# Seven-product matrix multiplication in another order: low halves last, one more chunk by seven products, and more low parts fetched by DMA

## The chip, the core and the metric

The kernel runs on one core of a Trainium2 chip. The core has five engines, each with an in-order stream of instructions of its own: TensorE (matrix products; in the profile PE, its weight loads PEld), VectorE (DVE), ScalarE (ACT), GpSimd (POOL) and SyncE (SP, which here only issues DMAs). They work side by side and wait for each other by semaphores. The metric is the device time of one execution in microseconds; lower is better.

## The reference

A trunk of two layers over 512 tokens of width 1024: layer 0 mixes tokens by gated linear attention, layer 1 by softmax attention. After each comes the part that the change is about:

```python
def conv_ffn(h, w_up, w_conv, b_conv, w_down):      # h 512 x 1024, w_up 1024 x 5632, w_down 2816 x 1024
    u = h @ w_up
    u = lax.conv_general_dilated(
        u, w_conv[:, None, :], window_strides=(1,), padding=[(1, 1)],
        dimension_numbers=('NWC', 'WIO', 'NWC'), feature_group_count=u.shape[-1]) + b_conv
    val, gate = jnp.split(u, 2, axis=-1)
    return (jax.nn.silu(gate) * val) @ w_down

...
        x = x + conv_ffn(rmsnorm(x, norm_ffn[i]), ffn_w_up[i], ffn_w_conv[i],
                         ffn_b_conv[i], ffn_w_down[i])
```

## The kernel before

**Numbers in two halves.** TensorE multiplies a reduced-precision type (fp32r). So every float32 operand is split into a high part, the value rounded to fp32r, and a low part, what is left. A product takes three matmuls: high weight by high input, high weight by low input, low weight by high input. `split` (L311 on) makes the high part on ScalarE (L319) and the low part on VectorE (L320). `low_dma` (L270 on) does it otherwise: ScalarE writes the high part (L271) and the negated value into the low tile (L272), and a DMA from GpSimd's queue adds the original values to it. The DMAs wait in `self.pending` until `flush` (L304 on) issues them (L308). Their source is the tile in the core's own memory or, where `home` is given, the same values in HBM.

**Pieces of weights.** The weights of a feed-forward layer are read in pieces of 128 x 1024 (512 KB) by SyncE. `W.todo` lists them in order; `made` holds those already split. `piece` flushes, makes what it was asked for if that has not been done, then makes up to `ahead` pieces in advance (`PA` = 4, or `PAW` = 6 from chunk 1 to chunk 19, when the tiles of x lend their space) and returns the one asked for. The program only states dependences and an order of writing; the order in which each engine gets its instructions is settled by a scheduler when the kernel is built.

**Chunks.** The 22 chunks of the up projection have 128 values and 128 gates each: two tiles of 128 x 512 results. In a plain chunk (`plain_up`, L1041) each tile is 8 x 3 matmuls of 512 columns. In the chunks of `SEVEN` the two tiles together are computed by Winograd's form of Strassen's scheme: seven products in place of eight, on blocks of half the size. `product` (L1065) is one of the seven: four block pairs, three matmuls of 256 columns each (L1074). Products 1 to 7 use sums of weight blocks, which `summed` (L275 on) makes: the first piece of a strip (half 0) is the stored one and serves products 1 and 4, the second (half 1: L293, L294) serves 6 and 2, the third 7 and 5, and the fourth, of half the size (L283 to L286), serves 3. `LOW_0` lists the chunks whose first piece gets its low part by `low_dma` out of HBM; elsewhere `split` makes it.

**Order of a chunk by seven products** (`seven_up`, L1083). Product 1 goes to a bank of its own (r1 in `pt`) and ScalarE doubles it (`twice`, L1129) into the bank `both`; the chunk pauses there until its predecessor has come far enough. Then: product 6 on top in r2; a copy of r2 to the first half of r3 (L1095, or L1204 in the down projection); product 7 to r4, doubled to `d`; product 4 on top of r3's first half; product 5 on top of r2; a copy of r2 to r3's second half (L1102, L1211); the sum of `d` and r3 on VectorE (L1132), which is the gate tile. Then product 1 of the next chunk, products 2 and 3, and the value tile is `both` itself. `act_up` (L1110) takes each tile through the convolution (L1117 to L1119), SiLU (L1121) and their product (L1122).

**The down projection** works in two parts of four strips (`down_part`, L1182) after chunks 9 and 17 (`DOWN_AFTER`), with the same products in the same order; its results are added to x in HBM by GpSimd's DMAs (`xd`). The rest of it (chunks 16 to 21, `PLAIN`) runs as plain products at the end. `prepare` (L1141 to L1157) builds the sums of the activations for it, for each pair of chunks up to 15.

**At the head of each feed-forward layer** the first three chunks use inputs not yet divided by the norm; `rescale` (L1029) prepares the others: xr (L1035), its high part nh, its low part nl by `low_dma` with xr as source.

Of the kernel before, what the change touches and what calls it, by code (L numbers as in the profile page):

```python
# [14 lines left out]
P = 128  # L15
# [54 lines left out]
SEVEN = (6, 7, 8, 10, 11, 12, 13, 15, 16, 18, 19, 20, 21)  # L70
UPA = 3
PA = 4
# [5 lines left out]
LOW_0 = (7, 8)  # L78
# [22 lines left out]
def hybrid_encoder_kernel(  # L101
# [74 lines left out]
    class Weights:  # L176
# [127 lines left out]
        def flush(self):  # L304

            for lo, r in self.pending:
                same = lo.dtype == F32R and r.dtype != F32R
                pool.dma_start(lo.bitcast(F32) if same else lo, r, accum_op=ALU.add)  # L308
            self.pending = []
# [40 lines left out]
    def add_ffn(layer):  # L350
        first = 0
        for m, part in DOWN_AFTER.items():
# [3 lines left out]
            W.todo[at : at + 2] = W.todo[at + 1], W.todo[at]  # L356
# [660 lines left out]
    def ffn(layer, norm, cw, nxt):  # L1017
# [11 lines left out]
        def rescale():  # L1029

            for p in range(KC // 2):
# [5 lines left out]
                W.low_dma(hi, lo, xr)  # L1037
                scaled.append(xr)
                fresh.extend((hi[:, i * S : (i + 1) * S], lo[:, i * S : (i + 1) * S]) for i in range(2))

        def plain_up(m):  # L1041

            pss = []
            for t in range(2):
# [3 lines left out]
                if t == 0 and m not in DOWN_AFTER:  # L1048
                    begin_up(m + 1)
                if t == 0 and m in DOWN_AFTER:  # L1050
                    down.append(down_part(DOWN_AFTER[m], m))
                    next(down[-1])
# [12 lines left out]
        def product(pieces, src, strip, pairs, i, dst, start):  # L1065
            h, o = PLACE[i]
            if h not in pieces:
                pieces[h] = W.piece(src, strip, h, PAW if W.wide else PA)
            wh, wl = pieces[h]
            for j, p in enumerate(pairs):  # L1070
                sl = slice(o + j * P, o + (j + 1) * P)
                mh, ml = p[i]
                for a, (w, m) in enumerate(((wh, mh), (wh, ml), (wl, mh))):
                    mm(dst, w[:, sl], m, start=start and j == 0 and a == 0, stop=j == len(pairs) - 1 and a == 2,  # L1074
                       skip_group_check=True)
# [6 lines left out]

        def seven_up(m):  # L1083
# [3 lines left out]
            r = bank("pt", "r1")[:, :H]  # L1087
            go(1, r, True)
            both = bank("acc", "r")
            r1, r2 = both[:, :H], both[:, H:]  # L1090
            twice(both, r)
            yield
            go(6, r2, False)
            r3 = bank("s", "r3")
            act.activation(r3[:, :H], r2, AF.Copy)  # L1095
# [6 lines left out]
            act.activation(r3[:, H:], r2, AF.Copy)  # L1102
            add_seven(d, r3, r4)
            yield 1, d
            begin_up(m + 1)
            go(2, r1, False)
# [75 lines left out]
        def down_part(part, m):  # L1182
# [6 lines left out]
            go = lambda n, *a: product(pieces[n], w_dn, part * NQ + n, pairs, *a)  # L1189

            def begin(n):
# [407 lines left out]
```

## Time and profile before

| | us |
|---|---|
| median of 3 runs | 1087.01 |
| lowest and highest | 1086.85, 1087.84 |
| span of the profiled execution, first to last instruction | 1085.5 |
| TensorE busy | 1077.5 |
| VectorE busy | 888.5 |
| ScalarE busy | 721.1 |
| GpSimd busy | 136.7 |

The profile is one execution recorded by the hardware. A group's row gives line, engine, operation, output and inputs by the program's names, shapes and count, then after a bar the busy time in us and the mean in ns of one, and after a second bar the idle time of the engine before them and what ended it. A row of waits says which engine waited at which line for which other, the total in us, the number of times and the longest. A row of a timeline has the start and the length in us, and in brackets the engine's idle time before it. Matmuls run into each other: the recorded length of one is more than the step to the next. Feed-forward layer 0 runs from 217.9 to about 562 us of the span, layer 1 from 735.7 us to the end. TensorE's granted clock is full (1.00) but for the last stretch.

### The profile page before, as it was taken

Reading aid. Unit: us, or ns where it says so; the run is one execution under the profiler, and the core shown is the slowest. Engines: PE = TensorE matmul, PEld = TensorE weight load, DVE = VectorE, ACT = ScalarE, POOL = GpSimd, SP = SyncE. Lnnn points to the kernel's source line nnn. Section 1 sums busy time; section 2 is a strip of 40 time slices with the busy share of each in tenths; the row PEclk is TensorE's granted clock in tenths of the full one; section 3 lists DMA queues with packets and bytes.
Section 4 is the critical chain, followed back from the end, with each engine's and each line's share of the span. In section 5 each row is a group of like instructions: output and inputs, shape, how many; then the busy total and the mean of one; then the engine's idle time right before and its main releaser. Section 6 shows DMA issues by size and latency. Waiting matters only on the chain.

```text
span 1085.5 us, 17391 instructions
## 1 busy us (share of the span) xinstructions
PE 1077.5 (99%) x6672; PEld 966.4 (89%) x6672; DVE 888.5 (82%) x1327; ACT 721.1 (66%) x1134; POOL 136.7 (13%) x153
## 2 busy tenths in 40 slices
PE   9999999999999999999999999999999999999998
PEld 8888988888999999999988888888889999999997
DVE  7998967569898899988755588666989889998882
ACT  8679575478775676666574677656877567666660
POOL 0212112021001100010015333002110010001000
PEclk9999999999999999999999999999999999999999
DMA  8744446499545633274767475549863473227542
GB/s 301 187 126 106 122 141 215 154 207 204 127 125 127 145 120 111 77 177 121 252 149 162 127 204 164 164 158 202 206 148 124 105 166 116 100 80 157 136 175 78
DMA packets 55763, 164.52 MB, mean 152 GB/s; under 512 B 6528, under 2 KB 7040, under 8 KB 55680
## 3 DMA queue, kind: packets, MB, share of 16 engines
q1 hardware_dynamic: 36192, 112.66, 32.2%
q0 software_dynamic: 14592, 42.21, 21.7%
q10 hardware_dynamic: 4896, 8.55, 2.1%
q8 instruction: 52, 0.85, 0.3%
q14 instruction: 31, 0.25, 0.1%
HBM read 114.89 MB, written 14.68 MB: 119 GB/s over the span
## 4 chain that ended last, share of the span: by engine, by line
PE 87%; DVE 6%; ACT 3%; DMA 2%; issue 2%; POOL 0%; SPq 0%; DVEq 0%; ACTq 0%; POOLq 0%
PE r L1074 37%; PE op L535 8%; PE vg L652 7%; PE up L482 4%; PE up L483 4%; PE up L484 4%; PE dn L483 2%; PE dn L484 2%; PE dn L482 2%; PE av L509 1%; PE A L482 1%; DVE wl L320 1%; PE A L484 1%; DMA nl<-xr 1%; PE B L484 1%
## 5 line engine op out<-in xcount | busy, mean ns | idle before, releaser
L320 DVE TENSOR_TENSOR wl<-raw,wh 128x1024 fp32r<-128x1024 f32 x156 | 189.8, 1220 | 31.3 <-ACT wh L319 31.1
L319 ACT ACTIVATE wh<-raw 128x1024 fp32r<-128x1024 f32 x156 | 162.6, 1053 | 73.4 <-PE op L535 20.7
L1074 PE MATMUL r<-gu,wh 128*128 128x256 f32 x896 | 161.2, 282 | 0.0
L1074 PE MATMUL r<-xt,wh 128*128 128x256 f32 x832 | 151.1, 283 | 0.4 <-ACT r L1095 0.3
L1074 PEld LDWEIGHTS r<-gu,wh 128*128 128x128 f32 x896 | 139.3, 190 | 1.0 <-ACT r L1211 0.2
L1074 PEld LDWEIGHTS r<-xt,wh 128*128 128x128 f32 x832 | 129.2, 190 | 1.6 <-ACT r L1095 1.1
L1074 PE MATMUL r<-gu,wl 128*128 128x256 f32 x448 | 126.3, 283 | 0.0
L1074 PE MATMUL r<-xt,wl 128*128 128x256 f32 x416 | 117.2, 283 | 0.0
L1074 PE MATMUL r<-nh,wh 128*128 128x256 f32 x312 | 88.8, 285 | 0.3 <-ACT r L1102 0.3
L1074 PE MATMUL r<-nh,wl 128*128 128x256 f32 x312 | 88.2, 283 | 0.0
L1074 PE MATMUL r<-nl,wh 128*128 128x256 f32 x312 | 87.9, 282 | 0.0
L1074 PEld LDWEIGHTS r<-gu,wl 128*128 128x128 f32 x448 | 85.1, 190 | 0.0
L1074 PEld LDWEIGHTS r<-xt,wl 128*128 128x128 f32 x416 | 79.1, 190 | 0.0
L482 PE MATMUL up<-nh,wh 128*128 128x512 f32 x192 | 75.3, 392 | 0.0
L483 PE MATMUL up<-nl,wh 128*128 128x512 f32 x192 | 75.2, 392 | 0.0
L484 PE MATMUL up<-nh,wl 128*128 128x512 f32 x192 | 75.2, 392 | 0.0
L535 PE MATMUL op<-oT,wh 128*128 128x512 f32 x256 | 72.4, 393 | 0.0
L271 ACT ACTIVATE wh<-raw 128x1024 fp32r<-128x1024 f32 x36 | 38.0, 1056 | 38.2 <-PE up L483 11.5
L1074 PEld LDWEIGHTS r<-nh,wh 128*128 128x128 f32 x312 | 59.3, 190 | 2.9 <-ACT r L1102 2.6
L1074 PEld LDWEIGHTS r<-nl,wh 128*128 128x128 f32 x312 | 59.4, 190 | 0.2
L1074 PEld LDWEIGHTS r<-nh,wl 128*128 128x128 f32 x312 | 59.4, 190 | 0.0
L535 PEld LDWEIGHTS op<-oT,wh 128*128 128x128 f32 x256 | 47.4, 188 | 9.7 <-ACT oT L937 0.3
(299 smaller groups left out, 2761.6 us busy)
## 6 DMA issues: line engine op xcount, KB each, us to landing
raw<-in_w_up_dram SPq DMA_DIRECT2D x84, 512.0 KB, 4.6
raw<-in_w_down_dram SPq DMA_DIRECT2D x44, 512.0 KB, 3.7
wl<-raw POOLq DMA_DIRECT2D x20, 512.0 KB, 5.3
wl<-in_w_up_dram POOLq DMA_DIRECT2D x16, 512.0 KB, 7.8
ring<-p ACTq DMA_DIRECT2D x32, 256.0 KB, 2.6
xw<-in_xw_dram SPq DMA_DIRECT2D x8, 512.0 KB, 6.6
raw<-in_w_v_dram SPq DMA_DIRECT2D x8, 512.0 KB, 5.9
raw<-in_w_g_dram SPq DMA_DIRECT2D x8, 512.0 KB, 4.0
```

Of the source, the lines that this page charges most:

```text
L271: act.activation(hi, r, AF.Copy)
L319: act.activation(hi[:, sl], a, AF.Copy)
L320: dve.tensor_tensor(lo[:, sl], a, hi[:, sl].bitcast(F32), ALU.subtract)
L482: mm(ps, wh, mh, start=start, stop=False)
L483: mm(ps, wh, ml, start=False, stop=False)
L484: return mm(ps, wl, mh, start=False, stop=stop)
L509: mm(ps[j][:, :width], hl[k][i == 2][:, j * P : (j + 1) * P], (wl if i == 1 else wh)[:, sl], start=k == 0 and i == 0, stop=k == KC - 1 and ...
L535: mm(pss[ng][n], wt[:, sl], mv, start=k == late[0][0] and i == 0, stop=k == late[-1][-1] and i == 2)
L652: last = mm(ps[j], m[:, js], w[:, sl], start=i in (1, 7, 2) and p == 0 and a == 0, stop=i in (4, 2, 3) and p == 3 and a == 2, skip_group_c ...
L1074: mm(dst, w[:, sl], m, start=start and j == 0 and a == 0, stop=j == len(pairs) - 1 and a == 2, skip_group_check=True)
```

## The change

Four things are changed, all in the feed-forward layers.

1. `product` runs its matmuls in another order: first both matmuls with the high weight for all four block pairs, then the four with the low weight. A copy out of the product's bank (`then`) is written straight after the matmuls, and only after it the making of further pieces, which had stood before them.
2. The seven products run in the order 1, 6, 7, 2, 5, (product 1 of the next chunk or strip), 4, 3 in place of 1, 6, 7, 4, 5, (next 1), 2, 3.
3. Chunk 14 joins `SEVEN` (its weights are laid out for it in HBM as those of the others), and chunks 11 to 16 join `LOW_0`.
4. `rescale` issues the DMAs of the low parts one by one, each behind the last DMA that had been sent before.

```diff
-SEVEN = (6, 7, 8, 10, 11, 12, 13, 15, 16, 18, 19, 20, 21)
+SEVEN = (6, 7, 8, 10, 11, 12, 13, 14, 15, 16, 18, 19, 20, 21)
...
-LOW_0 = (7, 8)
+LOW_0 = (7, 8, 11, 12, 13, 14, 15, 16)
...
-                pool.dma_start(lo.bitcast(F32) if same else lo, r, accum_op=ALU.add)
+                self.sent = pool.dma_start(lo.bitcast(F32) if same else lo, r, accum_op=ALU.add)
...
         def rescale():
 
+            W.flush()
+            sent = W.sent
             for p in range(KC // 2):
...
                 W.low_dma(hi, lo, xr)
+                with tc.issue_after(sent.ins):
+                    W.flush()
...
-        def product(pieces, src, strip, pairs, i, dst, start):
+        def product(pieces, src, strip, pairs, i, dst, start, then=None):
             h, o = PLACE[i]
             if h not in pieces:
-                pieces[h] = W.piece(src, strip, h, PAW if W.wide else PA)
+                pieces[h] = W.piece(src, strip, h, 0)
             wh, wl = pieces[h]
-            for j, p in enumerate(pairs):
-                sl = slice(o + j * P, o + (j + 1) * P)
-                mh, ml = p[i]
-                for a, (w, m) in enumerate(((wh, mh), (wh, ml), (wl, mh))):
-                    mm(dst, w[:, sl], m, start=start and j == 0 and a == 0, stop=j == len(pairs) - 1 and a == 2,
-                       skip_group_check=True)
+            steps = [(j, wh, a) for j in range(len(pairs)) for a in range(2)]
+            steps += [(j, wl, 0) for j in range(len(pairs))]
+            for n, (j, w, a) in enumerate(steps):
+                mm(dst, w[:, o + j * P : o + (j + 1) * P], pairs[j][i][a], start=start and n == 0,
+                   stop=n == len(steps) - 1, skip_group_check=True)
+            if then is not None:
+                then()
+            W.ahead((PAW if W.wide else PA) - len(W.made))
             W.flush()
...
+        def begin(m):
+            if m in DOWN_AFTER:
+                down.append(down_part(DOWN_AFTER[m], m))
+                next(down[-1])
+            else:
+                begin_up(m + 1)
+
         def seven_up(m):
...
-            go(6, r2, False)
             r3 = bank("s", "r3")
-            act.activation(r3[:, :H], r2, AF.Copy)
+            go(6, r2, False, copy(r3[:, :H], r2))
             r4 = bank("pt", "r4")[:, :H]
-            go(7, r4, True)
             d = tmp("u", "u")
-            twice(d, r4)
+            go(7, r4, True, lambda: twice(d, r4))
+            go(2, r1, False)
+            go(5, r2, False, copy(r3[:, H:], r2))
+            begin(m)
             go(4, r3[:, :H], False)
-            go(5, r2, False)
-            act.activation(r3[:, H:], r2, AF.Copy)
             add_seven(d, r3, r4)
             yield 1, d
-            begin_up(m + 1)
-            go(2, r1, False)
             go(3, r2, False)
             yield 0, both
```

`down_part` is changed in the same way; there the sum `f` of a strip is appended to `W.pending` after product 4 of that strip. `copy(o, i)` is ScalarE's copy of i to o.

More of the change, by code (lines that the diff above doesn't have):

```diff
@@ L1047, in plain_up @@
                 pss.append(ps)
[L1048 to L1052 removed]
+                if t == 0:
+                    begin(m)
                 if m == 0 and t == 0:
```

42 lines of the change are left out of this document (19 added, 23 removed).

## The prediction

> **What bounds the kernel now.** I read the page first: span, busy line, chain.
>
> ```profile
> span 1085.5 us, 17391 instructions
> ...
> PE 1077.5 (99%) x6672; PEld 966.4 (89%) x6672; DVE 888.5 (82%) x1327; ACT 721.1 (66%) x1134; POOL 136.7 (13%) x153
> ...
> PE 87%; DVE 6%; ACT 3%; DMA 2%; issue 2%; POOL 0%; SPq 0%; DVEq 0%; ACTq 0%; POOLq 0%
> ```
>
> TensorE has work for 99% of the span and carries 87% of the chain that ended last. Matmuls overlap, so busy time does not say how dense they are. The chain in order of time does: a piece's length by its count is the step from one matmul to the next.
>
> ```profile
> 187.83 30.26 PE op L535 x133
> ...
> 328.18 75.90 PE r L1074 x636
> ...
> 847.23 76.13 PE r L1074 x636
> ```
>
> L1074 is the matmul of the products, 256 columns: 75.90/636 = 119.3 ns, in layer 1 119.7 ns. A plain projection moves 512 columns; chunk 14's own matmuls, from the TensorE timeline (first and last of 13 in a row):
>
> ```profile
> 409.42 0.39 PE L484 MATMUL up<-nh,wl 128*128 128x512 f32 x1
> ...
> 412.14 0.39 PE L484 MATMUL up<-nh,wl 128*128 128x512 f32 x1
> ```
>
> 2.72 us over 12 steps: 226.7 ns. Neither step can be shortened by the other engines; all that can go is matmuls and the pauses between them. The waits of the weight loads list the pauses in the products:
>
> ```profile
> PEld r L1074 <- ACT r L1102: 2.6, 10, 0.5
> ...
> PEld r L1074 <- ACT r L1095: 1.1, 3, 0.7
> ...
> PEld r L1074 <- ACT r L1211: 0.2, 1, 0.2
> ```
>
> Fourteen waits, 3.9 us, all for ScalarE's copies inside PSUM (L1095 after product 6, L1102 and L1211 after product 5). A weight load runs ahead of its matmul, so not all of it is lost. Two stretches of chunks 6 to 8, layer 0 and layer 1, show what is; first all instructions, then those of L1074 alone (columns: window, its length, PE busy with count, PEld, DVE, ACT, POOL, clock, DMA share, GB/s):
>
> ```profile
> 286.40:315.90 29.50, 29.50 (x241) 28.89 (x240) 27.06 (x38) 21.86 (x34) 0.87 (x1) 1.00 0.44 126
> ...
> 804.30:835.00 30.70, 30.00 (x241) 28.98 (x241) 28.26 (x39) 23.77 (x37) 0.87 (x1) 1.00 0.50 145
> ```
>
> ```profile
> 286.40:315.90 29.50, 28.97 (x237) 28.46 (x237) 1.00 0.44 126
> 804.30:835.00 30.70, 29.19 (x236) 28.44 (x237) 1.00 0.50 145
> ```
>
> Layer 0: 237 x 0.1193 + 4 x 0.2267 = 29.2 of 29.5 us, 0.3 lost. Layer 1: 236 x 0.1193 + 5 x 0.2267 = 29.3 of 30.7, 1.4 lost. How such a pause comes about, ScalarE's and TensorE's timelines in layer 1:
>
> ```profile
> 826.20 1.06 ACT L319 ACTIVATE wh<-raw 128x1024 fp32r<-128x1024 f32 x1 [1.75 <-DMA raw<-in_w_up_dram]
> ...
> 828.53 0.37 ACT L1095 ACTIVATE r<-r 128x256 f32<-128x256 f32 x1
> ```
>
> ```profile
> 828.21 0.40 PE L482 MATMUL up<-nh,wh 128*128 128x512 f32 x1
> 828.95 0.51 PE L1074 MATMUL r<-xt,wh 128*128 128x256 f32 x2 [0.34 <-ACT r L1095]
> ```
>
> ScalarE, in order, waited for a load, then cut that piece, and the 0.37 us copy came late. Product 4 needs it one product (1.43 us) after product 6. A plain matmul (828.21) was fitted in, so the issued order is not the written one.
>
> **The change, part by part.** *Chunk 14 by seven products.* Per layer 48 matmuls go, 48 x 0.2267 = 10.88 us, and 7 x 4 x 3 = 84 come, 84 x 0.1193 = 10.02: -0.86, for two layers **-1.7 us**, all on the path. The Trainium skill (TensorE: Matmul & The Clock Gate, "Back-to-back issue gap") speaks against this step: it gives a stream of load and matmul about 81 ns at 128 columns and 131 at 512. Read off between them, 256 columns would take an estimated 98 ns, and seven products cost 84 x 98 - 48 x 131 = 1.9 us more per layer, 5.6 us worse over both than my sum. The trace disagrees with both figures (119.3 and 226.7 ns).
>
> The halving also costs other engines:
>
> ```profile
> L320 DVE TENSOR_TENSOR wl<-sum,wh 128x1024 fp32r<-128x1024 f32 x42 | 51.3, 1221 | 4.4 <-ACT wh L319 4.4
> L293 DVE TENSOR_TENSOR sum<-raw,raw 128x1024 f32<-128x1024 f32 x42 | 51.2, 1218 | 0.0
> ...
> L286 DVE TENSOR_TENSOR wl<-raw,wh 128x512 fp32r<-128x512 f32 x42 | 28.9, 688 | 17.7 <-PE r L1074 17.6
> L283 DVE TENSOR_TENSOR raw<-raw 128x512 f32<-128x512 f32 x42 | 28.8, 687 | 0.3
> L294 DVE TENSOR_TENSOR raw<-raw,sum 128x512 f32<-128x512 f32 x42 | 28.8, 686 | 0.4
> ...
> L285 ACT ACTIVATE wh<-raw 128x512 fp32r<-128x512 f32 x42 | 26.3, 627 | 7.9 <-DVE raw L283 7.7
> ...
> L1129 ACT ACTIVATE r<-r 128x512 f32<-128x512 f32 x42 | 24.4, 580 | 15.9 <-PE r L1074 15.7
> ...
> L1132 DVE TENSOR_TENSOR u<-u,r 128x512 f32<-128x512 f32 x26 | 17.7, 682 | 0.0
> ```
>
> VectorE per layer, with the first low part by DMA: 1.22 (L293) + 0.69 (L294) + 0.69 (L283) + 0.69 (L286) + 0.68 (L1132) = +3.97; the two large low parts that stay are as many as the plain chunk's. *The low part by DMA* takes 1.22 us (L320) from VectorE in each of the five other chunks: -6.10. Net **-2.1 us of VectorE per layer**, and by the time chunk 14 is prepared chunks 11 to 13 have given back 3.66 of its 3.97. That matters, because VectorE is full there:
>
> ```profile
> 363.80:405.80 42.00, 42.00 (x351) 41.70 (x350) 39.65 (x55) 30.27 (x49) 1.73 (x2) 1.00 0.44 125
> 405.80:438.40 32.60, 32.60 (x231) 30.46 (x230) 32.60 (x46) 20.92 (x33) 0.00 (x0) 1.00 0.36 114
> ```
>
> (39.65 of 42.0 us in chunks 10 to 13, 32.60 of 32.60 in 14 to 16.) On ScalarE each of six pieces gains a second pass (798.63 below), 6 x 1.04 = 6.2 us per layer, and chunk 14 one more large cut (1.05, row 363.01 below), a half one (0.63), two doublings (0.58) and two copies (0.37): 3.6 us; 30.27 and 20.92 us of 74.6 become about 61: hidden, unless it delays copies. GpSimd gains 12 issues and the queue 12 x 512 KB out of HBM. Their lead, from the same kind of piece in chunk 7 of layer 1, and from chunk 11's first piece of layer 0 as it is now:
>
> ```profile
> 797.68 1.04 ACT L271 ACTIVATE wh<-raw 128x1024 fp32r<-128x1024 f32 x1
> 798.63 1.04 ACT L272 ACTIVATE wl<-raw 128x1024 fp32r<-128x1024 f32 x1
> ```
>
> ```profile
> 799.97 0.87 POOL L308 DMA_DIRECT2D wl<-in_w_up_dram  x1 [3.45 <-ACT wl L272]
> ```
>
> ```profile
> L308 POOL DMA_DIRECT2D wl<-in_w_up_dram x2: 868/870/871, 800.0 to 808.4; - x2
> ...
> DMA to landing us min/median/max: 5.8/6.3/6.8
> ```
>
> ```profile
> 363.01 1.05 ACT L319 ACTIVATE wh<-raw 128x1024 fp32r<-128x1024 f32 x1
> ```
>
> ```profile
> 373.84 0.28 PE L1074 MATMUL r<-nh,wh 128*128 128x256 f32 x1
> ```
>
> Chunk 7's issue comes 2.29 us after its high part starts. So chunk 11's would come at 365.3; with low halves last its low part is first read eight matmuls into product 1, at 373.84 + 8 x 0.119 = 374.8. The transfer has 9.5 us and takes 5.8 to 6.8: cost nothing, 2.7 us to spare. That cover is gone if the pieces are made later or landings lengthen. The Trainium skill (SBUF — State Buffer, the "DVE blocks DMA" trap) warns that GpSimd's descriptors stand still while VectorE holds the port they share; by that rule the landing would be late and rival (b) below would come true. Issues of 868 to 871 ns beside a VectorE busy 28.26 of 30.70 us show nothing of it.
>
> *The order of the products.* Counts of matmuls and weight loads stay. Low halves last leaves fewer changes of operand, and the step may change: L535 loads another weight block for every matmul and steps at 30.26/133 = 227.5 ns, chunk 14's plain ones use a block twice and step at 226.7. The difference is 0.8 ns; on 3528 + 168 matmuls that bounds the effect at -3.0 to +3.0 us. I take 0, as here block and pair are kept. Product 6's copy now meets its first user, product 5 (it overwrites what the copy reads), after 7 and 2: 2.87 us in place of 1.43. That ends the L1095 kind. Product 5's copy is used by product 3 as before, after two products inside a run, after one (1.43 us) at a run's end; there only its place ahead of the next piece's cutting helps, and one run end of four (13) vanishes. So the 1.1 us of L1095 go, and of L1102's and L1211's 2.8 a fifth: 0.5. **-1.6 us**; ends 0 and -3.9. What is late next is the copy at the run ends, 8, 16 and 21.
>
> *Later sums.* A chunk's first sum moves behind product 4, two products (2.87 us) later, and both tiles' convolutions come closer together. The DMA that adds a down part's f moves too, on GpSimd's queue between chunk 11's low part and the DMA of g. Nothing on TensorE waits for either within a chunk of 10 us, as PSUM has three buffers of that bank. After chunk 21 the 16 units of chunks 16 to 19 cover the chain: 48 x 0.2267 = 10.9 us. Without cover it would cost up to 2.87 us per layer; I take 0.
>
> *The flush in rescale.* Four DMAs per layer are placed behind the last one sent.
>
> ```profile
> POOL nl L308 <- ACT nl L272: 13.2, 6, 2.9
> ```
>
> GpSimd stood waiting for ScalarE's low parts six times of eight, so its order was not what made them late: 0; ends -0.2 and +0.5 by one short issue.
>
> **Sum:** -1.7 - 1.6 = -3.3 us, span 1082.2. The executions' median is 1087.01, 1.5 us above the profiled span; the same distance gives **1083.7 us**.
>
> **The rivals.** *(a) The pauses only move.* ScalarE gets 9.8 us more work per layer, and its copies wait behind a second pass of 1.04 us. For: 826.20 above. Against: it stays near 80% busy there and the slack doubles. Then only chunk 14 counts: 1087.0 - 1.7 = 1085.3. The change not doing what it says, because the order is not issued as written, ends here too.
>
> *(b) Slower: the low part lands late.* Place: the first product of chunks 11 to 16; it decides when issue to landing exceeds 9.5 us, or 8.1 if the making slips one product. For it:
>
> ```profile
> nl<-xr POOLq DMA_DIRECT2D x8, 512.0 KB, 8.1
> ```
>
> That is the same size, where the queues are busier. Against: DMA share 0.36 to 0.44 in this stage. One microsecond late, twelve times: +12, so 1083.7 + 12 = 1095.7; half a microsecond gives 1089.7.
>
> *(c) VectorE becomes the bound in chunks 14 to 16.* If the relief of 11 to 13 is spent before chunk 14, its 3.97 us show on TensorE in each layer: 1083.7 + 7.9 = 1091.6. For: 32.60 of 32.60. Against: the relief is larger and earlier.
>
> *(d) Short matmuls don't pay.* Chunk 14 loses where 84 short steps outlast 48 long ones, from 226.7 x 48 / 84 = 129.5 ns on; at 150 ns it costs 84 x 0.150 - 10.88 = +1.7 us per layer: 1087.0 + 3.4 - 1.6 = 1088.8. No row of the products' chain comes near. (The Trainium skill's figures in TensorE: Matmul & The Clock Gate, weighed above, would bring this about.)
>
> *(e) All pauses go,* and the step gains a little: -1.7 - 3.9 = 1081.4.
>
> **How the numbers follow.** Forecast 0.54 (own range 1082.3 to 1084.8), (e) 0.10, (a) 0.21, (b) 0.09, (c) 0.05, (d) 0.01. Faster means by over 0.2%, below 1084.8, about what a measurement of this kernel tells from no change; slower is above 1089.2. Faster: forecast and (e), 0.64. Same: (a), (d) and 0.02 of (b) and (c), 0.24. Slower: the rest of (b) and (c), 0.12. The range for 8 in 10 leaves out the far end of (e) and most of (b) and (c): 1081.5 to 1087.2.
>
> **What would show it.** Right: 6744 matmuls (6672 - 96 + 168), L1074's step at 119 to 120 ns, no wait for product 6's copy, a few for product 5's at 8, 16 and 21; 12 more low parts by DMA, landing before product 1's ninth matmul; VectorE about 4 us less busy. Wrong: weight loads waiting for a DMA (b), or for the low parts of VectorE around 400 to 435 us (c); a step of 121 ns, 1.5 above the present one, which on 3696 matmuls costs 5.5 us by itself.

## The result and the profile after

The change makes the kernel slower. Before and after ran on the same chip.

| | before | after |
|---|---|---|
| median, us | 1086.93 (4 runs) | 1115.39 (4 runs, 1113.81 to 1117.82) |
| ratio, 95% interval | 1 | 1.0264 [1.0250, 1.0277] |
| span of the profiled execution | 1085.5 | 1113.4 |
| granted TensorE clock, mean | 1.000 | 0.994 |

The forecast was 1083.7, the range ended at 1087.2, and faster had been given 0.64. What happened is rival (b), a late low part, and beside it a smaller loss that the forecast had counted as a gain.

The page of the kernel after: span, busy line, chain.

```profile
span 1113.4 us, 17691 instructions
...
PE 1086.1 (98%) x6744; PEld 975.1 (88%) x6744; DVE 885.4 (80%) x1327; ACT 738.4 (66%) x1158; POOL 147.2 (13%) x165
...
PE 78%; issue 9%; DVE 7%; DMA 3%; ACT 2%; POOL 1%; SPq 0%; DVEq 0%; POOLq 0%; ACTq 0%
```

The counts are the predicted ones: 6744 matmuls (72 more), 12 more issues on GpSimd. VectorE is 3.1 us less busy (4.2 predicted), ScalarE 17.3 us more (19.6 predicted). But TensorE carries 78% of the chain and no longer 87%, and DMA has come into it. The waits of the weight loads in the kernel after (total us, times, longest) say where:

```profile
PEld r L1075 <- DMA wl<-in_w_up_dram: 16.9, 7, 3.4
PEld up L485 <- DMA wl<-in_w_up_dram: 4.2, 1, 4.2
PEld r L1075 <- ACT r L1098: 3.2, 12, 0.5
PEld r L1075 <- ACT r L1197: 1.3, 6, 0.3
```

L1075 is now the matmul of the products, L485 the low matmul of a plain projection. Eight waits for low parts out of HBM, 21.1 us, where before has none. The copies (L1098 in the up products, L1197 in the down ones) are waited for 18 times, 4.5 us; before it was 14 times and 3.9.

**Where.** Seven of the eight waits lie in layer 1: six for the first pieces of chunks 11 to 16, and one for chunk 2's second tile (L485). Chunk 11's wait as a window of the kernel after (window, its length, PE busy with count, PEld, DVE, ACT, POOL, clock, DMA share, GB/s):

```profile
900.90:903.90 3.00, 0.30 (x4) 0.10 (x2) 0.00 (x0) 0.50 (x1) 0.00 (x0) 1.00 1.06 214
```

In these 3.0 us TensorE, VectorE and ScalarE hardly work, with the DMA engines full.

**What a wait costs besides.** Behind four of the waits (chunks 2, 12, 14 and 15) the granted clock falls to half for 3.41 us. For three of them (chunks 2, 12 and 15) the next rows show the 3.41 us ahead of the fall and the 3.41 us at half clock; the row from 919.69 shows the clock back at full, and the last row, at chunk 16's wait, is a stretch that no fall follows:

```profile
772.91:776.32 3.41, 1.12 (x5) 0.95 (x6) 2.73 (x4) 0.59 (x1) 0.00 (x0) 1.00 1.04 308
776.32:779.73 3.41, 3.41 (x10) 2.62 (x9) 1.44 (x4) 3.41 (x5) 0.86 (x1) 0.50 0.35 118
...
912.86:916.27 3.41, 1.30 (x11) 1.10 (x10) 2.77 (x4) 0.73 (x2) 0.00 (x0) 1.00 0.70 162
916.27:919.68 3.41, 3.03 (x14) 3.04 (x15) 0.00 (x0) 1.18 (x3) 0.00 (x0) 0.50 0.14 54
919.69:923.10 3.41, 3.41 (x30) 3.41 (x30) 2.57 (x4) 3.30 (x4) 0.87 (x1) 1.00 0.09 10
...
953.82:957.23 3.41, 0.22 (x3) 0.02 (x2) 2.39 (x4) 0.37 (x1) 0.00 (x0) 1.00 0.77 189
957.23:960.63 3.40, 3.40 (x16) 3.40 (x17) 0.00 (x0) 0.58 (x1) 0.00 (x0) 0.50 0.12 51
967.47:970.88 3.41, 1.66 (x14) 1.66 (x15) 3.41 (x7) 1.78 (x3) 0.00 (x0) 1.00 0.79 228
```

Taken as lost time that is at most 4 x 3.41 x 0.5 = 6.8 us on top of the waits. By the trace's record of the granted clock it changes at 776.32, 779.74, 916.27, 919.68, 943.58, 946.99, 957.23 and 960.64, always a whole number of 3.413 us apart (1, 40, 1, 7, 1, 3, 1 of them). So there is a grid of steps of 3.413 us that no wait sets anew. A step is followed by one at half clock when TensorE was busy for 0.22 to 1.35 us of it here (1.35 ahead of 943.58; 1.60 in e7 below, from 430.36), and not when it was for 1.66 us (1.74 in e12, from 407.54). Chunk 11's wait lies across two steps and leaves TensorE busy for more than that in each, so it costs no clock. The Trainium skill (TensorE: Matmul & The Clock Gate, "What's actually happening") says that the clock is halved after an idle window of about 3.4 us that runs freely; the trace agrees in the length and in that the windows run freely, but here a window that is idle for about half of it is enough.

**How one is late.** Chunk 11's first piece in layer 1 of the kernel after, on ScalarE (the cut L271, the second pass L272; the last row is chunk 12's cut), on GpSimd, and on TensorE at product 1:

```profile
892.76 1.04 ACT L271 ACTIVATE wh<-raw 128x1024 fp32r<-128x1024 f32 x1
893.71 1.04 ACT L272 ACTIVATE wl<-raw 128x1024 fp32r<-128x1024 f32 x1
...
905.59 1.06 ACT L271 ACTIVATE wh<-raw 128x1024 fp32r<-128x1024 f32 x1 [0.37 <-PE r L1075]
```

```profile
895.04 1.04 POOL L308 DMA_DIRECT2D wl<-in_w_up_dram  x1
...
907.89 0.87 POOL L308 DMA_DIRECT2D wl<-in_w_up_dram  x1 [10.91 <-ACT wl L272]
```

```profile
900.89 0.28 PE L1075 MATMUL r<-nl,wh 128*128 128x256 f32 x1
903.86 0.74 PE L1075 MATMUL r<-nh,wl 128*128 128x256 f32 x4 [2.70 <-DMA wl<-in_w_up_dram]
```

The issue comes 2.28 us after the cut starts, as predicted (2.29). But the low part is due at 900.89 + 0.12 = 901.01, 5.97 us after the issue, not 9.5; and it lands at about 903.8, 8.8 us after it. Chunk 12's cut (905.59) waits for TensorE: for product 4 of chunk 10, which held the buffer.

The same for all six, worked out from the trace of after (lead: issue to the first low matmul had it not waited; landing: issue to landing; us):

| chunk | 11 | 12 | 13 | 14 | 15 | 16 |
|---|---|---|---|---|---|---|
| layer 0, lead | 6.0 | 8.6 | 9.4 | 9.3 | 6.9 | 8.1 |
| layer 0, landing | 5.7 | 5.4 | 5.8 | 5.6 | 5.9 | 5.6 |
| layer 1, lead | 6.0 | 6.1 | 6.2 | 4.5 | 5.7 | 2.4 |
| layer 1, landing | 8.8 | 8.7 | 7.7 | 6.8 | 9.0 | 5.6 |

The profile's list of DMA issues in the kernel after, for these six in layer 0 and in layer 1 (the last number is the median from issue to landing):

```profile
wl<-in_w_up_dram POOLq DMA_DIRECT2D x6, 512.0 KB, 5.7
...
wl<-in_w_up_dram POOLq DMA_DIRECT2D x6, 512.0 KB, 8.2
```

Same transfers, same order of the products, two layers: in layer 1 they have less lead and land later. What differs between the layers is who lends the buffers:

```
def two(self):
    self.turn += self.wide
    if self.wide and self.turn % 3 == 0:
        return pair("x", KC // 2, F32R, "wh"), pair("x", KC // 2, F32R, "wl")
    return pair("wh", NH, F32R, "wh"), pair("wl", NL, F32R, "wl")
```

Every third pair made while `wide` is set comes out of x's tiles, which hold two pairs, and `turn` runs on from layer 0 into layer 1. A layer makes 76 such pairs before the change and 77 after it, since chunk 14 has one more; chunk 10's first is the 31st of its layer. Layer 0: 31 leaves 1, so the third piece of chunks 10 to 16 (33, 36, ...) gets x; before, with chunk 14 plain, of chunks 10 to 13. Layer 1 before: 76 + 31 = 107, so the second piece of chunks 10 to 13. Layer 1 after: 77 + 31 = 108, so the **first** piece. The first pair of layer 1, now the 78th, is that of chunk 2's second piece; it gets x too, and its low part, issued at 753.22 in e1 below, is issued at 767.19. The first piece's pair is held until product 4, last but one of a unit in the new order, so the first piece of the chunk after next can be cut only five products, 7.2 us, ahead of its use.

### The profile page after: what moved, and what is told of

Its sections match the earlier page's. It is cut to its first block, busy times and chain, and to the rows that moved or that the text cites. A ratio compares the mean times of both kernels' runs of the same rounds, so it can differ in the third digit from the quotient of the medians.

```text
span 1113.4 us, 17691 instructions
## 1 busy us (share of the span) xinstructions
PE 1086.1 (98%) x6744; PEld 975.1 (88%) x6744; DVE 885.4 (80%) x1327; ACT 738.4 (66%) x1158; POOL 147.2 (13%) x165
## 4 chain that ended last, share of the span: by engine, by line
PE 78%; issue 9%; DVE 7%; DMA 3%; ACT 2%; POOL 1%; SPq 0%; DVEq 0%; POOLq 0%; ACTq 0%
PE r L1075 33%; PE op L536 8%; PE vg L653 7%; PE up L485 3%; PE up L483 3%; PE up L484 3%; PE dn L484 2%; PE dn L483 2%; PE dn L485 2%; DMA wl<-in_w_up_dram 2%; DVE wl L320 1%; PE av L510 1%; PE A L483 1%; DVE xr L1038 1%; PE A L485 1%
## 5 line engine op out<-in xcount | busy, mean ns | idle before, releaser
L320 DVE TENSOR_TENSOR wl<-raw,wh 128x1024 fp32r<-128x1024 f32 x144 | 175.0, 1218 | 38.0 <-ACT wh L319 37.7
L1075 PE MATMUL r<-xt,wh 128*128 128x256 f32 x896 | 129.6, 287 | 0.3
L1075 PE MATMUL r<-gu,wh 128*128 128x256 f32 x896 | 126.7, 283 | 0.1
L1075 PEld LDWEIGHTS r<-xt,wh 128*128 128x128 f32 x896 | 117.9, 194 | 3.0 <-ACT r L1098 2.2
L1075 PEld LDWEIGHTS r<-gu,wh 128*128 128x128 f32 x896 | 115.6, 190 | 2.5 <-ACT r L1197 1.3
L1075 PE MATMUL r<-nh,wh 128*128 128x256 f32 x336 | 84.8, 284 | 0.3 <-ACT r L1098 0.3
L1075 PE MATMUL r<-nl,wh 128*128 128x256 f32 x336 | 84.2, 283 | 0.0
L271 ACT ACTIVATE wh<-raw 128x1024 fp32r<-128x1024 f32 x48 | 50.6, 1054 | 37.8 <-PE op L536 7.9
L1075 PE MATMUL r<-xt,wl 128*128 128x256 f32 x448 | 72.5, 284 | 0.0
L1075 PE MATMUL r<-gu,wl 128*128 128x256 f32 x448 | 71.4, 283 | 0.0
L1075 PE MATMUL r<-nh,wl 128*128 128x256 f32 x336 | 55.8, 288 | 15.5 <-DMA wl<-in_w_up_dram 15.5
L1075 PEld LDWEIGHTS r<-nh,wh 128*128 128x128 f32 x336 | 64.3, 191 | 1.3 <-ACT r L1098 0.9
L1075 PEld LDWEIGHTS r<-nl,wh 128*128 128x128 f32 x336 | 64.3, 191 | 0.1
L485 PE MATMUL up<-nh,wl 128*128 128x512 f32 x160 | 62.6, 391 | 0.0
L1075 PEld LDWEIGHTS r<-xt,wl 128*128 128x128 f32 x448 | 62.2, 193 | 0.0
L1075 PEld LDWEIGHTS r<-nh,wl 128*128 128x128 f32 x336 | 47.0, 194 | 16.9 <-DMA wl<-in_w_up_dram 16.9
L1075 PEld LDWEIGHTS r<-gu,wl 128*128 128x128 f32 x448 | 61.4, 191 | 0.1
L308 POOL DMA_DIRECT2D wl<-in_w_up_dram x28 | 24.6, 879 | 255.7 <-ACT wl L272 181.7
```

The costliest lines, as they stand in the source:

```text
L271: act.activation(hi, r, AF.Copy)
L308: self.sent = pool.dma_start(lo.bitcast(F32) if same else lo, r, accum_op=ALU.add)
L320: dve.tensor_tensor(lo[:, sl], a, hi[:, sl].bitcast(F32), ALU.subtract)
L485: return mm(ps, wl, mh, start=False, stop=stop)
L1075: mm(dst, w[:, o + j * P : o + (j + 1) * P], pairs[j][i][a], start=start and n == 0, stop=n == len(steps) - 1, skip_group_check=True)
```

## The experiments

Theories: **T1**, the turn makes layer 1's low parts late. **T2**, transfers land late in layer 1 whatever the buffer. **T3**, the new order holds the first piece too long whatever the buffer. A loss outside these waits is looked for with them: the **bank theory** is introduced below. "Pauses" in the tables is worked out from each trace in the same way: over the steps that lead to a matmul of the products, what a step over 150 ns has beyond 119.5 ns (behind a plain matmul: beyond 226.7 ns), summed by layer. Before: 0.8 and 2.5 us; after: 4.8 and 23.2, of which 3.9 are steps at half clock. (Some expectations quote a rougher first count: 4.6 and 1.6 for e4, and for before 3.3 in layer 1, which is both layers together.)

### The turn

*e1_phase*, the changed kernel with the turn started anew:

```diff
-                W.loads, W.wide = LOADS_FFN, 1
+                W.loads, W.wide, W.turn = LOADS_FFN, 1, 0
```

> The changed kernel (1115.4 us), but the count that lends every third pair of a piece's halves the buffers of x starts anew in each layer, so that layer 1 lends them to the third piece of chunks 10 to 16, as layer 0 does, and not to the first. Theory T1 (the late low parts of layer 1 come from that turn: with the first piece in x's two pairs it can be made only some 7 us ahead of its use): the weight loads' waits for a DMA (15.5 + 3.7 us) fall to about what layer 0 has, under 1.5 us, the granted clock goes back to 1.00, and the time falls by these 19 us and up to 7 of slower clock: 1088 to 1097. Rival T2 (the transfers of layer 1 land in 7 to 9 us, whatever the buffer): the waits stay above 10 us and the time above 1108. Rival T3 (the new order holds the first piece too long, whatever the buffer): the same, above 1108.

1091.29 us, ratio 1.0038 [1.0023, 1.0053]; clock 1.000; pauses 4.8 and 4.7. One number, 24.1 us. Weight loads' waits:

```profile
PEld r L1075 <- ACT r L1098: 4.2, 16, 0.5
PEld r L1075 <- ACT r L1197: 1.4, 6, 0.3
...
PEld r L1075 <- DMA wl<-in_w_up_dram: 0.9, 2, 0.5
```

*e2_swap*, the turns of the layers exchanged:

```diff
-                W.loads, W.wide = LOADS_FFN, 1
+                W.loads, W.wide, W.turn = LOADS_FFN, 1, 0 if W.turn else 2
```

> The changed kernel with the turns of the two layers exchanged: layer 0 lends x's buffers to the first piece of chunks 10 to 16, layer 1 to the third. T1: the stalls move to layer 0: product 1 of chunks 11 to 16 waits there 1.5 to 3.5 us each for a low part out of HBM, and in layer 1 under 0.5 each; the time stays within 1105 to 1120. T2: the stalls stay in layer 1, and layer 0 shows under 2 us of them in all. T3: both layers would stall, above 1130.

1117.68 us (one run), pauses 22.7 and 4.6: the stalls are in layer 0 now. The matmuls' waits, then the six transfers of layer 0 and of layer 1:

```profile
PE r L1075 <- DMA wl<-in_w_up_dram: 14.7, 6, 3.5
PE up L485 <- DMA wl<-in_w_up_dram: 5.1, 1, 5.1
```

```profile
wl<-in_w_up_dram POOLq DMA_DIRECT2D x6, 512.0 KB, 7.8
...
wl<-in_w_up_dram POOLq DMA_DIRECT2D x6, 512.0 KB, 5.8
```

T1 is shown from both sides. T2 falls: even the long landing goes with the turn. T3 falls as the whole cause.

*e3_nolow*, the changed kernel with its turn, without the new transfers:

```diff
-LOW_0 = (7, 8, 11, 12, 13, 14, 15, 16)
+LOW_0 = (7, 8)
```

> The changed kernel without the new transfers: the low part of the first piece of chunks 11 to 16 is cut by VectorE as before; chunk 14 stays by seven, the order stays new, and the turn stays that of the changed kernel. T1 and T2 alike: the 15.5 us of waits for a low part in chunks 11 to 16 go, with the clock's loss behind them; the 3.7 us of chunk 2's second tile stay, as its low part still comes by DMA into a buffer of x: 1092 to 1098. If the new order itself is the cost (first piece made too late for VectorE's cut too), it stays above 1103.

1099.80, ratio 1.0118 [1.0101, 1.0135], pauses 5.7 and 6.6: more than expected by 2 us. The transfers' waits are gone and chunk 2's 3.7 us stayed, as T1 says. But without the transfers the products pause for 12.3 us, where e1's pause for 9.5; among that are waits for low parts of VectorE (three, 1.1 us) and for a cut of ScalarE (one, 0.9 us), which e1 doesn't have.

### The order of the products

*e4_order*: the kernel after with `SEVEN` and `LOW_0` as before, so the order and the flush alone.

> The kernel before with the new order of the seven products and the flush in the rescaling alone: chunk 14 plain, no new transfers, the turn as before. By the prediction's terms (waits for copies -1.6 us, low halves 0): 1085.4, the ratio 0.9985. The changed kernel's layer 0 reads otherwise: it is 2.7 us longer with chunk 14's -0.86 in it, though almost nothing waits for a DMA there; if the order is the cause of that, twice 3.5 us: 1094, the ratio 1.006; if chunk 14 or the transfers are, 1085 to 1088.

1090.52, ratio 1.0030 [1.0018, 1.0042], pauses 4.7 and 1.8. The order costs 3.3 us where it should have given 1.6. The two copies share a line there, so one kernel more was made only to be read. *e9_lines* is e4 with lines of their own:

```diff
+                if i == 2:
+                    mm(*args, **rest)      # L1078
+                elif i == 5:
+                    mm(*args, **rest)      # L1080
+                elif i == 4:
+                    mm(*args, **rest)      # L1082
+                elif i == 3:
+                    mm(*args, **rest)      # L1084
...
-            go(5, r2, False, copy(r3[:, H:], r2))
+            go(5, r2, False, copy5(r3[:, H:], r2))
```

> The kernel with the new order alone (1090.5 us) with the matmuls of products 2, 5, 4 and 3 and the copy after product 5 on lines of their own; nothing else differs, so the time stays at 1089.5 to 1091.5. Bank theory: the weight loads that wait for the copy after product 6 are those of product 2, and those that wait for the copy after product 5 are those of product 4; product 5 and product 3 wait for neither more than once. The prediction's reading: product 5 waits for the copy after 6, product 3 for the copy after 5, and products 2 and 4 for none.

1091.28 (one run). Its weight loads' waits; L1108 and L1208 are the copies after product 6 (up, down), L1109 and L1209 those after product 5:

```profile
PEld r L1082 <- ACT r L1109: 2.2, 8, 0.4
...
PEld r L1082 <- ACT r L1209: 0.8, 4, 0.3
...
PEld r L1078 <- ACT r L1108: 0.8, 4, 0.2
PEld r L1078 <- ACT r L1208: 0.7, 3, 0.2
```

All nineteen waits are those of product 4 for the copy after 5 (12) and of product 2 for the copy after 6 (7); products 5 and 3 have none. Yet product 2 writes `r1`, and the copy reads `r2`: they share nothing but the bank `both`. Product 4 writes the first half of `r3`, the copy after 5 the second. The issued program keeps order by whole banks (the bank theory), or by whole tiles: each of these tiles is one bank, so the runs can't tell the two apart. The Trainium skill says why it must (PSUM — Partial Sum Buffer, "PSUM bank collisions raise a hardware error"): two engines in one bank and quadrant of partitions at a time raise an error, whatever the addresses, so a bank and not an address is to be guarded. The waits here agree with it; what happens without them no run here shows.

One such wait in e4, ScalarE and then TensorE:

```profile
373.12 1.04 ACT L319 ACTIVATE wh<-raw 128x1024 fp32r<-128x1024 f32 x1
374.06 0.36 ACT L1098 ACTIVATE r<-r 128x256 f32<-128x256 f32 x1
```

```profile
374.00 0.52 PE L1075 MATMUL r<-nh,wl 128*128 128x256 f32 x3
374.48 0.39 PE L1075 MATMUL r<-nh,wh 128*128 128x256 f32 x1
374.70 0.28 PE L1075 MATMUL r<-nl,wh 128*128 128x256 f32 x1
374.82 0.28 PE L1075 MATMUL r<-nh,wh 128*128 128x256 f32 x1
```

The copy stood behind a piece's cut (373.12) and ended at 374.42; product 2 starts at 374.48. Mark the second matmul: 0.22 us after the first, where the next takes 0.12. Behind each of e4's twelve steps of more than 0.26 us comes such a second step, 0.1 us more.

*e6_pairs* is e4 with high and low matmuls alternating as before; *e5_lowlast* is the kernel before with the reverse of this edit alone:

```diff
-            steps = [(j, wh, a) for j in range(len(pairs)) for a in range(2)]
-            steps += [(j, wl, 0) for j in range(len(pairs))]
+            steps = [(j, w, a) for j in range(len(pairs)) for w, a in ((wh, 0), (wh, 1), (wl, 0))]
```

> The kernel before with one thing of the change: within each product the four low matmuls come last. The order of the products, the places of the copies, chunk 14 and the transfers are as before. If low halves last are what costs the 3.3 us of the order (a product can then be cut in two by the issued order, so that less stands between a copy and its user): 1089 to 1091. If the order of the products and the copies' places are: 1086.5 to 1088.

> The new order of the products, with the new places of the copies, but high and low matmuls alternate as before; chunk 14 plain, no new transfers. If the waits go by banks (product 2 writes the bank whose other half the copy after product 6 reads, product 4 the bank into whose other half the copy after product 5 writes), the slack of each copy is one product as before, whatever the order: the waits for copies do not end, and the time is 1087 to 1091. If the prediction's reading were right (product 5 is the first user of product 6's copy), the waits for that copy end here: 1085 to 1086. If low halves last alone are the cost, 1087 at most.

e5: 1089.35, 1.0015 [1.0006, 1.0024], pauses 3.5 and 2.2. e6: 1090.26, 1.0026 [1.0016, 1.0035], pauses 4.0 and 1.6. Each half of the order costs by itself, 1.6 and 2.5 us against the runs of before beside them; together that is more than e4's 3.3. But the halves don't cost by the same waits. The weight loads of e6's products wait so:

```profile
PEld r L1074 <- ACT r L1097: 2.5, 9, 0.4
PEld r L1074 <- DMA wl<-in_w_up_dram: 1.3, 1, 1.3
```

The DMA is chunk 8's low part in layer 0, for which before doesn't wait: the new order starts the next unit before product 4, and so reads it earlier. By what ended each pause, before has 3.3 us, all for ScalarE; e5 5.7, all for copies; e6 5.6, of which 1.4 for that low part; e4 6.5, of which 0.8 for it. So by one trace each, low halves last lengthen the pauses for copies by 2.4 us, the order of the products by 0.9. Why low halves last alone do that isn't settled: products can then be issued in parts, but in e5's trace 273 of the 294 stand whole, eight high matmuls and four low ones.

*e11_two* puts two products behind the copy after 6, from the bank theory, on the kernel before (the down products alike):

```diff
             twice(both, r)
             yield
+            go(2, r1, False)
+            yield
             go(6, r2, False)
...
             twice(d, r4)
+            begin_up(m + 1)
             go(4, r3[:, :H], False)
             go(5, r2, False)
...
             yield 1, d
-            begin_up(m + 1)
-            go(2, r1, False)
+            second_up(m + 1)
             go(3, r2, False)
```

> The kernel before with another order, made from the bank theory: 6, copy, 7, the next unit's 1, 4, 5, copy, the next unit's 2, 3. So no matmul writes a bank that a copy still reads or writes until two products have passed after the copy behind 6 (7 and the next 1), and one after the copy behind 5 (the next 2). Bank theory: the waits for copies fall from 14 to under 7 and the time by 1 to 2 us: 1085 to 1086.5. If the waits come from ScalarE's cuts whatever the slack, or the pieces come later because two units hold theirs at once: 1087 or more.

1089.35, 1.0015 [1.0006, 1.0024]. The waits for copies fell to 8 (2.3 us), all for the copy after 5; those for the copy after 6 are gone, as the bank theory has it. But three for a doubling (1.7) and one for a low part out of HBM (1.2) came, and the gain was missed. That this order holds pieces longer is the likely reason; it wasn't tried apart.

### Chunk 14 and the transfers

On the kernel before, old order: *e7_chunk14* adds 14 to `SEVEN` and starts the turn anew as in e1; *e8_old* is e7 with `LOW_0` as in the change; *e10_low* has the new transfers alone (`LOW_0 = (7, 8, 11, 12, 13, 15, 16)`, turn as before).

> The kernel before with chunk 14 by seven products alone, in the old order, its first low part cut by VectorE, and the turn of x's buffers started anew in each layer so that adding a piece doesn't shift it. By the prediction's sum -1.7 us: 1085.3, the ratio 0.9984. By its rival (c), VectorE as the bound in chunks 14 to 16, which has no relief from chunks 11 to 13 here: up to +7.9 - 1.7: 1093.

> Chunk 14 by seven and the low parts of chunks 11 to 16 by DMA, both as in the change, in the old order of the products, with the turn started anew in each layer. T1 (the transfers are hidden where the first piece is made 10 us ahead): no wait for a DMA over 1 us, and what chunk 14 gives is kept: 1084.5 to 1086. If the transfers cost by themselves (ScalarE's second passes in front of the copies): 1086 to 1089. If the old order holds the pieces so that the transfers are late: above 1089.

> The kernel before with the new transfers alone, for chunks 11, 12, 13, 15 and 16 (14 stays plain), old order of the products, the turn as before (third piece in layer 0, second in layer 1). If the transfers are hidden wherever the first piece isn't in x's buffers, and what VectorE gives back (6.1 us per layer) is worth nothing while chunk 14 is plain: 1086.5 to 1088. If ScalarE's second pass in front of the copies costs: 1088 to 1091. If VectorE's relief ends some waits for copies: 1085 to 1086.5.

| | median | ratio, interval | pauses |
|---|---|---|---|
| e7 | 1096.43 | 1.0080 [1.0066, 1.0094] | 8.3, 6.7 |
| e8 | 1093.90 | 1.0057 [1.0044, 1.0070] | 6.1, 7.4 |
| e10 | 1088.74 | 1.0014 [1.0005, 1.0023] | 2.3, 2.0 |

e7 is rival (c) come true, above even its price. A window near chunk 16 of layer 0, then the longest of its matmuls' waits:

```profile
425.00:437.00 12.00, 9.77 (x66) 9.17 (x65) 12.00 (x18) 9.58 (x14) 0.00 (x0) 0.87 0.40 128
```

```profile
PE r L1074 <- ACT wh L319: 5.6, 6, 1.5
PE r L1074 <- ACT r L1095: 1.5, 4, 0.7
PE r L1074 <- ACT r L1211: 1.4, 2, 0.7
```

VectorE is busy for all 12 us, TensorE for 9.77: the sums come late, so ScalarE cuts late. The transfers give back 2.5 us of it (e8), but T1's expectation for e8 failed: the old order reads a low part at its third matmul, and e8 waits four times for one (3.5 us, up to 1.2) and twenty times for copies (8.0 us). With chunk 14 plain the transfers cost 1.1 us (e10), as had been expected if ScalarE's second pass stands in front of the copies: these are waited for 18 times, 4.8 us. In these runs VectorE's relief is worth something only where VectorE is late.

### Which turn

*e12_second* is the changed kernel with `W.turn = 1` in place of e1's 0 (second piece in x); *e13_oldsecond* the same on e8; *e14_pairs* is e12 with e6's loop; *e15_turn0* is the kernel before with e1's line alone; *e16_orderturn* is e4 with it, *e17_twoturn* e11 with it.

> The changed kernel with the turn of x's buffers started at 1 in each layer, so that the second piece of chunks 10 to 16 gets them, not the first (changed kernel, layer 1) or the third (layer 0 and e1). If the rest of the loss hangs on the turn (order alone: 4.6 us of pauses in the products of layer 0 with the third piece there, 1.6 in layer 1 with the second; e1: 4.7 and 4.7): pauses about 1.6 us in each layer, so 6 us less than e1: 1085 to 1087. If chunk 14 or the order make the pauses whatever the turn: 1090 to 1092, as e1. If chunks 7 and 8, whose first piece gets x's buffers by this turn, now wait for their low parts: above 1092.

> Chunk 14 by seven and the transfers in the old order, with the second piece in x's buffers in both layers. It differs from e8 (1093.9) by the turn alone and from e12 by the order alone. If the turn makes the pauses: 1086 to 1089. If the old order can't feed chunk 14, whatever the turn: 1092 to 1095.

> e12 with high and low matmuls alternating in the products, as before the change. If low halves last give the low parts the time they need (eight matmuls, 0.95 us): more waits for low parts than e12, 1 to 4 us slower than e12. If they only cut the products apart: 0 to 2 us faster than e12.

> The kernel before, with the turn started anew in layer 1 (third piece in x's buffers there, as in layer 0); nothing else. Its products pause for 0.8 us in layer 0 and 3.3 in layer 1: if the turn is what tells the layers apart in the old order, layer 1 falls to about 1 and the time to 1085 to 1086. If not: 1086.5 to 1088.5.

> The new order alone (e4, 1090.5), with the turn started anew in each layer, as in e1 (1091.3): e1 and this kernel differ by chunk 14 by seven and the new transfers only. If the pauses of the new order hang on the third piece being in x (4.6 us in layer 0 against 1.6 in layer 1 of e4): 1092.5 to 1094, and chunk 14 with its transfers is worth about -1.7 us, as the prediction had it. If they don't: 1090 to 1091, and chunk 14 with its transfers brings nothing or costs up to 1.

> The order of e11 (two products behind the copy after 6, 1089.4) with the turn of e15 (1085.7). If the turn alone makes layer 1's pauses and the order ends those for the copy after 6: 1084.5 to 1086. If this order too has its own waits (for a doubling, for chunk 7's or 8's low part): 1087 to 1090.

| | median | ratio, interval | pauses |
|---|---|---|---|
| e12 | 1102.32 | 1.0138 [1.0125, 1.0152] | 9.2, 9.2 |
| e13 | 1090.71 | 1.0033 [1.0021, 1.0044] | 4.3, 3.9 |
| e14 | 1095.23 | 1.0076 [1.0063, 1.0088] | 6.7, 6.2 |
| e15 | 1085.72 | 0.9990 [0.9981, 0.9999] | 1.4, 0.8 |
| e16 | 1093.22 | 1.0050 [1.0037, 1.0063] | 4.4, 5.1 |
| e17 | 1088.49 | 1.0009 [1.0000, 1.0018] | 2.5, 2.9 |

The expectation for e12 failed: the second piece in x is no cure. No wait for a DMA is left in its products, but copies are late by up to 2.4 us. ScalarE's timeline of e12 shows one, then its weight loads' waits:

```profile
405.53 1.06 ACT L319 ACTIVATE wh<-sum 128x1024 fp32r<-128x1024 f32 x1 [1.34 <-DVE sum L293]
...
408.82 1.04 ACT L271 ACTIVATE wh<-raw 128x1024 fp32r<-128x1024 f32 x1
409.76 1.04 ACT L272 ACTIVATE wl<-raw 128x1024 fp32r<-128x1024 f32 x1
...
411.23 0.36 ACT L1098 ACTIVATE r<-r 128x256 f32<-128x256 f32 x1
```

```profile
PEld r L1075 <- ACT r L1098: 12.8, 23, 2.6
```

ScalarE stood 1.34 us for a sum, then worked without a break through 5.7 us of cuts and other passes before it came to the copy. The second pass L272, which the prediction costed at nothing, stands in that queue. e14 is 7 us faster than e12, more than any expectation had it, as its copies are waited for 4.6 us and not 15.0. Yet it waits six times, 6.7 us, for low parts, where e12 waits for none: low halves last do give the low parts time, as the first expectation had it, but the copies lose more by it. e13 lies between its expectations: the turn takes 3.2 us off e8, and the old order with chunk 14 still costs 3.6. e15 to e17 came out as expected: for the turn (e15, e16), and for waits of its own in the order of e11 (e17). The turn acts in each order and to different sums; why just so wasn't followed further.

e15 is the fastest kernel of all: one line, 0.1% below before, with an interval that ends just under 1. e16 and e1 differ by chunk 14 and the transfers (and by what one more piece shifts in x's lending behind chunk 14): 1.0050 to 1.0038, or 1.9 us of medians, though the intervals overlap.

## Why the prediction was wrong, step by step

In one row, from before to after: 1087 -> order (e4) 1090.5 -> turn anew (e16) 1093.2 -> chunk 14 with transfers (e1) 1091.3 -> the turn as it is in the change 1115.4.

- **The low part's lead, "9.5 us", "cost nothing, 2.7 us to spare"**: the step that failed, with 24 of the 28 us. It was read from the old timeline of chunk 11 in layer 0. Its own condition, "gone if the pieces are made later or landings lengthen", was met on both sides. Even in layer 0 chunk 11's lead is 6.0 us: issued 2.1 us later than reckoned (367.4, not 365.3), and read 1.4 us earlier (373.4, not 374.8), as the new order starts the next unit before product 4; 0.3 us were left of 2.7. In layer 1 the turn shortened the other leads too (2.4 to 6.2 us) and lengthened the landings (to 9.0 us, where 5.8 to 6.8 had been taken from two transfers; the page before gives 7.8 as the median of all sixteen of this kind). That one more piece per layer shifts who gets x's buffers stood in the code and was not weighed.
- **Rival (b)** had the place and the mechanism, and its bound: late when landing exceeds lead. Its price (twelve times one microsecond) was missed in shape: six times 1.5 to 3.3 us, one of 3.7 to 4.2 in chunk 2 that it did not name, and half clock for 3.41 us behind four of them.
- **"Waits for copies -1.6 us"**: wrong in sign; the order as a whole costs 3.3 us (e4), low halves last and 0.8 us for chunk 8's low part among them. The failed sentence is "Product 6's copy now meets its first user, product 5 ..., after 7 and 2": the first user is product 2, by the bank, one product after, and product 4 became a second one for the copy after 5. "That ends the L1095 kind" failed with it.
- **Low halves last, 0 (ends -3.0 and 3.0)**: the step between matmuls stayed at 119 to 120 ns, as taken. But e5 costs 1.6 us, by pauses for copies, which that bound had not been made for; that it lies inside the ends is luck.
- **Chunk 14, -1.7 us**: stood for the matmuls. Take each span less its pauses, where the clock stayed at 1.00: with 14 plain 1081.9 to 1083.6, mean 1082.5 (before, e4 to e6, e9 to e11, e15 to e17); by seven, always with the transfers, 1079.8 to 1080.7, mean 1080.3 (e1, e8, e12 to e14). That is 2.2 us less. What chunk 14 lost, it lost in pauses. The Trainium skill's issue gaps, by which it would have cost 5.6 us more, are not borne out.
- **VectorE's relief and rival (c)**: right in mechanism; without the transfers, in the old order and with the turn anew, chunk 14 costs 8.7 us (e7). The relief gave back only 2.5 of that there (e8); with the new order chunk 14 and the transfers together bring 1.9 (e16 to e1).
- **ScalarE's 9.8 us per layer, "hidden, unless it delays copies"**: the size was about right (17.3 for two layers, 19.6 reckoned), and they do delay copies (e10, e12).
- **The trap of the shared port**, weighed for rival (b): the landings were late, but not by it, as the last section shows.
- **Later sums and the flush, 0**: not tried apart. No wait for either shows in e1.

## What to carry to other kernels

A transfer that is "hidden" is hidden by a lead, and the lead has to be worked out again in the changed order and for every layer or pass: issue, landing and first use each move. A pool that is dealt out by a running count is part of the schedule; adding one piece anywhere shifts who gets which buffer everywhere behind it, so reset the count where the pattern repeats, and choose where it starts by measuring: the same reset gained 1.4 us in the old order (e15) and cost 2.7 in the new one (e4 to e16). Reckon PSUM slack by banks, and count what is queued in front of the copy on its own engine.

## What the runs showed of the hardware

*Landing goes with what starts beside it, not with VectorE's load.* In the bad turn a low part is issued together with a load of a piece of weights; the kernel after, SyncE:

```profile
907.81 0.33 SPq L230 DMA_DIRECT2D raw<-in_w_up_dram  x1
```

GpSimd's issue of chunk 12's low part (907.89, above) is 0.08 us behind it, and it lands 8.7 us later. In e1 a load goes at 907.19 and the low part 2.15 us after it:

```profile
907.19 0.33 SPq L230 DMA_DIRECT2D raw<-in_w_up_dram  x1
```

```profile
909.34 0.87 POOL L308 DMA_DIRECT2D wl<-in_w_up_dram  x1 [8.92 <-ACT r L1098]
```

It lands 5.8 us after its issue. The 36 transfers for chunks 11 to 16 in after, e1 and e2 divide the same way: eight with a load at most 0.4 us from their issue land in 7.7 to 9.0 us, two with one 1.5 us ahead in 6.8 and 7.5, and the other 26, whose nearest load goes 2.0 us or more ahead or 1.6 us or more behind, in 5.4 to 6.0, chunk 16's of the bad layers (5.6 and 5.7) among them. So it goes with the shared start, and not with the layer or the turn as such; that the start is the cause was not tried by itself. The Trainium skill's "DVE blocks DMA" trap (SBUF — State Buffer) would put it down to VectorE holding the port that it shares with GpSimd; which operations here would do so no run shows. From issue to landing of chunk 11's low part in layer 1, after and then e1:

```profile
895.00:903.80 8.80, 6.17 (x52) 5.96 (x50) 4.58 (x5) 4.09 (x7) 1.97 (x3) 1.00 0.91 171
```

```profile
888.56:894.58 6.02, 6.02 (x51) 5.92 (x49) 4.48 (x7) 3.34 (x6) 2.60 (x3) 1.00 0.75 127
```

VectorE was busy 52% of the time of the late one and 74% of the punctual one, and the issues at 907.89 (late) and 909.34 (punctual) both took 0.87 us. The trace does not bear the trap out here.

*A pause costs more than its length*: 0.1 us on the matmul after the first, and, where it leaves TensorE busy for less than about half of one step of the clock's 3.413 us grid (1.60 us and under, in these traces), half the clock for the whole of the next step.
